# A decoder block's first conditioning columns loaded 256 wide, and its last addition and norm ordered by token tile

## The chip, the cores and the metric

The kernel runs on one core of a Trainium2 chip. The core has five engines that run side by side, each through its own instructions in order: TensorE (PE: products of matrices, into PSUM), VectorE (DVE), ScalarE (ACT), GpSimd (POOL) and SyncE (SP), which here issues most transfers. Sixteen DMA engines carry the transfers. The metric is the time of one execution on the device in microseconds (us), lower is better.

## The reference

The function is one block of a decoder on 512 tokens of 1024 channels, in float32, with a conditioning vector `c`:

```
mod = silu(c) @ w_ada + b_ada                      # 6 rows of 1024: sh1, sc1, g1, sh2, sc2, g2
h   = layer_norm(x) * (1 + sc1) + sh1
mix = hybrid_mixer(h, w_in, ...)                   # h @ w_in, state-space scan, short convolution, gates, w_o
x   = layer_norm(ALPHA * x + g1 * mix) * ln1_g + ln1_b
h   = layer_norm(x) * (1 + sc2) + sh2
ffn = moe_ffn(h, ...)                              # 64 experts, 8 per token, and one shared expert
x   = layer_norm(ALPHA * x + g2 * ffn) * ln2_g + ln2_b
```

The change touches the first two lines, as far as `sh1` and `sc1` go, and the last one.

## The kernel before

**Start.** The tokens are four tiles of 128 (`xt`), the channels eight chunks of 128. `x` is normed by token tile (`ln_stats`, L189 to L195, L258), and transposed by chunk. Before a chunk k can be scaled and shifted, its 128 columns of `sh1` and `sc1` must be known. `ada_cols(k)` loads these columns of `w_ada`, two tiles of 1024 x 128 (SP, L183, 512 KB each). `ada_mm(k)` multiplies them (L286): `csz` holds silu(c) in column 0 of 32, and the eight row blocks go to four groups of 32 columns of the array, each into its own 32 partitions of PSUM, so four products run side by side. ScalarE copies the result (L289). `h_chunk(k)` adds up the partitions with a product by ones (L294), adds the bias (L295), transposes the four token tiles (L150), scales and shifts (L300, into `hr`), splits `hr` into a rounded part and the rest (L158, L160), and multiplies it by the narrow columns for dt (L306, for two chunks at a time). The split parts feed `matmul3`, three products (L153 to L155) of a chunk of h with a chunk of four tiles of `w_in` (`first`), which are loaded and split beforehand. The loop runs over the eight chunks and keeps ada_mm and h_chunk one chunk ahead of the products.

Tiles of 1024 numbers per partition ("pages") come from 14 slots; a load waits until a slot is free. `am2` is one PSUM bank whose halves serve chunks in turn.

**Order.** A planner sets the order of the instructions on each engine from the program's order, its own costs and the times at which it expects operands; each engine then runs through its list in order. Only for TensorE in the expert stage the order is that of the program (`manual_schedule`).

**End.** The experts follow the mixer in units. The products of a unit's last block are added to the result `ra` by `csteps`, for the four token tiles in two halves of 512 columns (L1188 and L1189 into PSUM, L1194 adds; the last time L1191, which also gives the row sums). Before the change `combine(True)` runs all eight additions, and `finish` then norms: for each token tile a square with its sum (`square`: L1483 on VectorE, L1484 on ScalarE), the root (`root`: L1488, L1489) and the scaling and the store (`scale`: L1497 and L1498 on VectorE; for tile 0 L1492 on ScalarE and L1501, L1502 on GpSimd; the store at L1503). `FORD` is their order in the program. After that a loop for overflowing experts (L1510) follows, which makes no pass here; it holds a second call of both.

Of the kernel before, what the change touches and what calls it, by code (L numbers as in the profile page):

```python
# [8 lines left out]
F32 = mybir.dt.float32  # L9
# [4 lines left out]
OP = mybir.AluOpType  # L14
# [28 lines left out]
NDEF = 2  # L43
FORD = "q0 r0 s0 q1 r1 s1 q2 r2 s2 q3 r3 s3"
NADA = 3
# [18 lines left out]
def block_kernel(ctx: ExitStack, tc: tile.TileContext, a, out, dbg=None):  # L64
# [164 lines left out]

    def ada_cols(k):  # L230
        ws = []
        for i in range(2):
            ws.append(load_cols(a["w_ada"][0], i * D + k * P))
        return ws

    first = [C_X, C_X + P, C_B, C_C]
    awt = {0: ada_cols(0), 1: ada_cols(1)}
    wdt = work.tile([P, KD, NH], F32, name="wdt")
# [30 lines left out]
    dtp = bank("y", 2)  # L269
    am2 = bank("y", 2)  # L270
    fw, hrs = {}, {}
    ams = {}

    def ada_mm(k):
        if k + 2 < KD:
            awt[k + 2] = ada_cols(k + 2)
        if k == 0:
            win_load(first[2])
            win_load(first[3])
        am = am2[:, k % 2 * 256:k % 2 * 256 + 256]  # L280
        ws = awt.pop(k)
        for i in range(2):
            for half in range(2):
                for j in range(4):
                    kk = half * 4 + j
                    PE.matmul(am[32 * j:32 * j + 32, i * P:(i + 1) * P], csz[:, kk, :], ws[i][:, kk, :],  # L286
                              start=(half == 0), stop=(half == 1), tile_position=(0, 32 * j))
        ams[k] = wk()
        S.activation(ams[k][:, :256], am, AF.Copy)  # L289

    def h_chunk(k):
        am = am2[:, k % 2 * 256:k % 2 * 256 + 256]
        for i in range(2):
            PE.matmul(am[:, i:i + 1], ams[k][:, i * P:(i + 1) * P], ones[:, 0:1], start=True, stop=True)  # L294
        V.tensor_tensor(m1[:, k, :], am[:, :2], bcol[:, :, k], op=OP.add)  # L295
        tp = bank("tr", 2)
        for t in range(NT):
            transpose(tp[:, t * P:(t + 1) * P], xt[t][:, k * P:(k + 1) * P])
        hr = wk()
        V.tensor_scalar(hr, tp, m1[:, k, 1:2], m1[:, k, 0:1], op0=OP.mult, op1=OP.add)  # L300
        split_to(hh(k), hl(k), hr)
        hrs[k] = hr
        if k % DTG == DTG - 1:
            for q in range(k - DTG + 1, k + 1):
                j = q % 4
                PE.matmul(dtp[32 * j:32 * j + 32, :], wdt[:, q, :], hrs.pop(q), start=(q < 4), stop=(q >= 4),  # L306
                          tile_position=(0, 32 * j))
# [3 lines left out]
    for k in range(KD):  # L311
        if k + 1 < KD:
            ada_mm(k + 1)
        for i, c0 in enumerate(first):
# [881 lines left out]

    def combine(last=False):
        for _ in csteps(last):
            pass


# [208 lines left out]
    def unit(n):  # L1410
# [17 lines left out]
        drain(run)  # L1428

    over_ = iter(())  # L1430
    need_x(1)
# [4 lines left out]
    with tc.manual_schedule(engines={mybir.EngineType.PE}):  # L1436
        for n in range(MAN, len(units)):
            unit(n)
        combine(True)
    ostart, oend, obase, nov = far  # L1440
# [30 lines left out]

    ln2g, ln2b = page([D]), page([D])
    SY.dma_start(ln2g, bc_rows(a["ln2_g"], D))
    SY.dma_start(ln2b, bc_rows(a["ln2_b"], D))

    def finish():

        os_, st = {}, {}

        def square(t):  # L1480
            os_[t] = page([D])
            st[t] = const.tile([P, 4], F32, name="fst", bufs=4)
            V.tensor_scalar(st[t][:, 0:1], rsum[:, t, 0:1], rsum[:, t, 1:2], -1.0 / D, op0=OP.add, op1=OP.mult)  # L1483
            S.activation(os_[t], ra[t], AF.Square, bias=st[t][:, 0:1], scale=1.0, accum_out=st[t][:, 1:2])  # L1484

        def root(t):
            nmu, ss, rs, nb = (st[t][:, i:i + 1] for i in range(4))
            S.activation(rs, ss, AF.Sqrt, bias=epsc, scale=1.0 / D)  # L1488
            V.reciprocal(rs, rs)  # L1489
            if ENG3[t] != "VV":  # L1490
                V.tensor_tensor(nb, nmu, rs, op=OP.mult)
                S.activation(os_[t], ra[t], AF.Identity, bias=nb, scale=rs)  # L1492

        def scale(t):
            o, nmu, rs = os_[t], st[t][:, 0:1], st[t][:, 2:3]
            if ENG3[t] == "VV":
                V.scalar_tensor_tensor(o, ra[t], nmu, ln2g, op0=OP.add, op1=OP.mult)  # L1497
                V.scalar_tensor_tensor(o, o, rs, ln2b, op0=OP.mult, op1=OP.add)  # L1498
            else:
                e1, e2 = ({"V": V, "P": GP}[e] for e in ENG3[t])  # L1500
                e1.tensor_tensor(o, o, ln2g, op=OP.mult)  # L1501
                e2.tensor_tensor(o, o, ln2b, op=OP.add)  # L1502
            SY.dma_start(out[0, t * P:(t + 1) * P, :], o)  # L1503

        for c in FORD.split():
            {"q": square, "r": root, "s": scale}[c[0]](int(c[1]))

    finish()
    nv = nc.values_load(nov[0:1, 0:1], min_val=0, max_val=E + 32)
    with tc.For_i(0, nv, 1):  # L1510
# [3 lines left out]
        drain(expert([[0]], [[0]], [blk], [xsplit(blk[0])], lambda e, q: expert_piece(bass.ds(er, 1), q)))  # L1514
        combine(True)
        finish()
# [25 lines left out]
```

## Time and profile before

| | |
|---|---|
| time, three runs | median 1582.76 us (1582.29 to 1587.55) |
| profiled execution | 1580.36 us, span 1578.6 us |
| TensorE busy | 1486.1 us, 94% |
| VectorE busy | 975.3 us, 62% |
| ScalarE busy | 644.8 us, 41% |
| GpSimd busy | 227.3 us, 14% |
| moved by DMA | 335.67 MB, mean 213 GB/s |

The profiled execution is a run of its own; the span is the part of it between the first and the last instruction. Busy times are the sums of the instructions' spans on each engine. PE is the engine's products, PEld its loading of weights, which goes on beside the products.

### The profile page before, as it was taken

How to read it: one execution, taken by the hardware profiler on the slowest of the kernel's cores; microseconds unless marked ns; L12 is line 12 of the kernel's file. 1: busy time of each engine (PE TensorE's matmuls, PEld its weight loads, DVE VectorE, ACT ScalarE, POOL GpSimd, SP SyncE). 2: the span in 40 equal slices, each digit the busy share in tenths (PEclk: the TensorE clock that was granted, in tenths of full speed). 3: DMA queues.
4: the chain of work that ended last, by engine and by line, in shares of the span. 5: the costliest groups of instructions: out<-in, count | busy, mean ns of one | idle time of the engine just before them, and what ended most of it. 6: DMA issues, size and time to landing. Idle time of an engine off the chain costs nothing.

```text
span 1578.6 us, 22869 instructions
## 1 busy us (share of the span) xinstructions
PE 1486.1 (94%) x8253; PEld 1010.2 (64%) x8253; DVE 975.3 (62%) x1810; ACT 644.8 (41%) x925; POOL 227.3 (14%) x232
## 2 busy tenths in 40 slices
PE   6999989999999999999988999999988999999994
PEld 3688777787787886788766455555555554454552
DVE  4457786678767666635696666454566544563456
ACT  3456665575643445523353333232343322231222
POOL 0011110111010445700023300000000000000001
PEclk9999999999999999999999999999999999999997
DMA  9763423632531557634622967998989788997871
GB/s 278 183 158 91 104 67 84 151 77 80 151 88 37 170 178 231 202 101 148 228 84 92 370 224 260 375 383 296 345 299 349 293 332 336 353 365 282 319 286 55
DMA packets 194504, 335.67 MB, mean 213 GB/s; under 512 B 13428, under 2 KB 136660, under 8 KB 186196
## 3 DMA queue, kind: packets, MB, share of 16 engines
q1 hardware_dynamic: 183300, 303.73, 55.6%
q0 software_dynamic: 11088, 30.45, 7.4%
q8 instruction: 66, 1.08, 0.3%
q14 instruction: 50, 0.41, 0.1%
HBM read 334.58 MB, written 4.28 MB: 215 GB/s over the span
## 4 chain that ended last, share of the span: by engine, by line
PE 73%; DMA 11%; DVE 8%; ACT 3%; issue 2%; POOL 1%; SPq 1%; DVEq 0%; ACTq 0%; POOLq 0%
PE ps_pj L153 12%; PE ps_pj L154 12%; PE ps_pj L155 12%; PE ps_pj L950 8%; DMA pr<-in_w_up_dram 8%; PE ps_y L950 5%; PE ps_y L1188 5%; PE ps_y L1189 5%; PE ps_tr L150 4%; DMA pg<-in_w_ada_dram 2%; DVE wl L160 2%; PE ps_y L153 1%; PE ps_y L155 1%; PE ps_y L154 1%; PE ps_y L483 1%
## 5 line engine op out<-in xcount | busy, mean ns | idle before, releaser
L153 PE MATMUL ps_pj<-hm,wh 128*128 128x512 f32 x680 | 276.5, 408 | 1.0 <-ACT wh L158 0.9
L155 PE MATMUL ps_pj<-hm,wl 128*128 128x512 f32 x680 | 267.7, 394 | 6.3 <-DVE wl L160 6.3
L154 PE MATMUL ps_pj<-hm,wh 128*128 128x512 f32 x680 | 267.7, 394 | 0.0
L160 DVE TENSOR_TENSOR wl<-pg,wh 128x1024 fp32r<-128x1024 f32 (+1 forms) x129 | 159.6, 1244 | 114.0 <-ACT wh L158 113.9
L950 PE MATMUL ps_pj<-pr,xt 128*32 128x512 f32 (+1 forms) x1472 | 214.2, 604 | 11.9 <-DMA pr<-in_w_up_dram 11.7
L158 ACT ACTIVATE wh<-pg 128x1024 fp32r<-128x1024 f32 (+1 forms) x135 | 127.5, 953 | 137.3 <-PE ps_pj L154 101.6
L950 PEld LDWEIGHTS ps_pj<-pr,xt 128*32 128x32 f32 (+1 forms) x1472 | 62.0, 117 | 153.2 <-issue 149.6
L153 PEld LDWEIGHTS ps_pj<-hm,wh 128*128 128x128 f32 x680 | 129.1, 190 | 36.3 <-issue 6.9
L155 PEld LDWEIGHTS ps_pj<-hm,wl 128*128 128x128 f32 x680 | 128.6, 189 | 35.9 <-DVE wl L160 8.1
L154 PEld LDWEIGHTS ps_pj<-hm,wh 128*128 128x128 f32 x680 | 128.8, 189 | 29.1 <-issue 3.4
L160 DVE TENSOR_TENSOR wl<-pr,wh 128x1024 fp32r<-128x1024 f32 x72 | 86.8, 1222 | 85.9 <-ACT wh L158 85.4
L1194 DVE TENSOR_TENSOR res<-res,ps_y 128x512 f32<-128x512 f32 x120 | 82.4, 687 | 76.0 <-PE ps_y L1189 74.4
L1132 POOL DMA_INDIRECT pg<-h_d,idx x41 | 45.4, 1107 | 559.6 <-DVE oht L1161 174.3
L158 ACT ACTIVATE wh<-pr 128x1024 fp32r<-128x1024 f32 x72 | 74.3, 1054 | 91.2 <-DMA pr<-in_w_up_dram 54.5
L950 PE MATMUL ps_y<-pr,wkr 128*32 128x512 f32 (+1 forms) x736 | 102.7, 596 | 1.3 <-DVE wk L1165 1.3
L927 ACT ACTIVATE sg<-ps_pj 128x256 f32<-128x256 f32 x44 | 16.8, 383 | 173.7 <-PE ps_pj L950 116.4
L928 DVE TENSOR_TENSOR sg<-sg,ps_pj 128x256 f32<-128x256 f32 x44 | 18.3, 420 | 111.8 <-ACT sg L927 111.8
L366 POOL TENSOR_TENSOR pg<-pg 128x1024 f32<-128x1024 f32 x28 | 73.8, 2650 | 56.9 <-ACT pg L364 56.8
L153 PE MATMUL ps_pj<-pg,wh 128*128 128x512 f32 x192 | 75.9, 395 | 1.1 <-ACT zs L431 1.1
L155 PE MATMUL ps_pj<-pg,wl 128*128 128x512 f32 x192 | 76.2, 397 | 0.0
L154 PE MATMUL ps_pj<-pg,wh 128*128 128x512 f32 x192 | 75.8, 395 | 0.0
L416 DVE SCALAR_TENSOR_TENSOR wk<-ps_pj,cw,wk 128x511 f32<-128x511 f32 (+2 forms) x93 | 68.3, 742 | 7.4 <-ACT wk L414 7.0
(394 smaller groups left out, 2658.5 us busy)
## 6 DMA issues: line engine op xcount, KB each, us to landing
pr<-in_w_gate_dram SPq DMA_DIRECT2D x128, 512.0 KB, 10.1
pr<-in_w_up_dram SPq DMA_DIRECT2D x128, 512.0 KB, 10.6
pr<-in_w_down_dram SPq DMA_DIRECT2D x64, 1024.0 KB, 9.6
pg<-in_w_in_dram SPq DMA_DIRECT2D x88, 512.0 KB, 6.4
pg<-in_w_ada_dram SPq DMA_DIRECT2D x48, 512.0 KB, 3.5
bc<-acs_d POOLq DMA_DIRECT2D x32, 256.0 KB, 4.1
pg<-in_w_ssd_out_dram SPq DMA_DIRECT2D x16, 512.0 KB, 4.4
pg<-in_w_sc_out_dram SPq DMA_DIRECT2D x8, 512.0 KB, 4.0
```

What stands on the lines that cost most here:

```text
L150: return PE.transpose(o, i, ident[:n, :n])
L153: PE.matmul(o, lh, rh, start=start, stop=False)
L154: PE.matmul(o, lh, rl, start=False, stop=False)
L155: PE.matmul(o, ll, rh, start=False, stop=stop)
L158: S.activation(hi, src, AF.Copy)
L160: V.tensor_tensor(lo, src, rw(hi), op=OP.subtract)
L366: GP.tensor_tensor(part[i], part[i], w, op=OP.add)
L416: V.scalar_tensor_tensor(acc[:, s:], o[:, :T - s], cw[:, 3 - s, tl:tl + 1], acc[:, s:], op0=OP.mult, op1=OP.add)
L950: PE.matmul(o[w * i:w * i + w, :], x[:, w * i:w * i + w], m, start=start, stop=stop, tile_position=(0, w * i))
L1188: PE.matmul(o, oh_, yh[:, ns_], start=(i == 0), stop=False)
L1189: PE.matmul(o, oh_, yl[:, ns_], start=False, stop=(i == len(ps_) - 1))
L1194: V.tensor_tensor(ra[t][:, ns_], ra[t][:, ns_], o, op=OP.add)
```

## The change

The columns of `w_ada` for `sh1` and `sc1` are loaded for two chunks at once: for each of the two parts and each half of the rows one tile of 512 x 256, so that one piece in memory is 1 KB instead of 512 B. `ada_mm` runs for pairs of chunks, with 256 columns in one product, into one whole PSUM bank. The loads of the third and fourth tile of `w_in` are issued ahead of those of the next pair. At the end, `finish` stands inside the stretch with TensorE's manual order and takes the additions as steps of its own (c0 to c3, two halves each); FORD puts the squares, roots and scalings of the token tiles between them. The loads of `ln2_g` and `ln2_b` are in `finish`, at its first call.

```diff
-FORD = "q0 r0 s0 q1 r1 s1 q2 r2 s2 q3 r3 s3"
+FORD = "c0 q0 r0 s0 c1 q1 r1 c2 q2 r2 s1 c3 q3 r3 s2 s3"
...
-    def ada_cols(k):
-        ws = []
+    def ada_cols(kp):
+
+        ws = {}
         for i in range(2):
-            ws.append(load_cols(a["w_ada"][0], i * D + k * P))
+            for half in range(2):
+                v = ws[i, half] = page([4, 256])
+                SY.dma_start(v, a["w_ada"][0, half * 512:half * 512 + 512, i * D + kp * 256:i * D + kp * 256 + 256]
+                             .rearrange("(k p) n -> p k n", p=P))
         return ws
...
-    awt = {0: ada_cols(0), 1: ada_cols(1)}
+    awt = {0: ada_cols(0)}
...
-    def ada_mm(k):
-        if k + 2 < KD:
-            awt[k + 2] = ada_cols(k + 2)
-        if k == 0:
+    def ada_mm(kp):
+        if kp == 0:
             win_load(first[2])
             win_load(first[3])
-        am = am2[:, k % 2 * 256:k % 2 * 256 + 256]
-        ws = awt.pop(k)
+        if 2 * kp + 2 < KD:
+            awt[kp + 1] = ada_cols(kp + 1)
+        ws = awt.pop(kp)
         for i in range(2):
             for half in range(2):
                 for j in range(4):
-                    kk = half * 4 + j
-                    PE.matmul(am[32 * j:32 * j + 32, i * P:(i + 1) * P], csz[:, kk, :], ws[i][:, kk, :],
+                    PE.matmul(am[32 * j:32 * j + 32, i * 256:(i + 1) * 256], csz[:, half * 4 + j, :], ws[i, half][:, j, :],
                               start=(half == 0), stop=(half == 1), tile_position=(0, 32 * j))
-        ams[k] = wk()
-        S.activation(ams[k][:, :256], am, AF.Copy)
+        ams[kp] = wk()
+        S.activation(ams[kp], am, AF.Copy)

     def h_chunk(k):
-        am = am2[:, k % 2 * 256:k % 2 * 256 + 256]
+        kp, c = k // 2, k % 2
+        sums = am[:, 2 * c:2 * c + 2]
         for i in range(2):
-            PE.matmul(am[:, i:i + 1], ams[k][:, i * P:(i + 1) * P], ones[:, 0:1], start=True, stop=True)
-        V.tensor_tensor(m1[:, k, :], am[:, :2], bcol[:, :, k], op=OP.add)
+            PE.matmul(sums[:, i:i + 1], ams[kp][:, i * 256 + c * P:i * 256 + c * P + P], ones[:, 0:1], start=True, stop=True)
+        V.tensor_tensor(m1[:, k, :], sums, bcol[:, :, k], op=OP.add)
...
-        if k + 1 < KD:
-            ada_mm(k + 1)
+        if k % 2 and k + 1 < KD:
+            ada_mm(k // 2 + 1)
...
+    def finish():
+
+        if not ln2:
+            for nm in ("ln2_g", "ln2_b"):
+                ln2.append(page([D]))
+                SY.dma_start(ln2[-1], bc_rows(a[nm], D))
+        ln2g, ln2b = ln2
+        com = csteps(True)
+        os_, st = {}, {}
+
+        def add(t):
+            next(com)
+            next(com)
...
+            {"c": add, "q": square, "r": root, "s": scale}[c[0]](int(c[1]))
...
     with tc.manual_schedule(engines={mybir.EngineType.PE}):
         for n in range(MAN, len(units)):
             unit(n)
-        combine(True)
+        finish()
...
-    finish()
     nv = nc.values_load(nov[0:1, 0:1], min_val=0, max_val=E + 32)
     with tc.For_i(0, nv, 1):
...
-        combine(True)
         finish()
```

`square`, `root` and `scale` are the same in both.

## Rows read from the trace of the kernel before

**Rows 1.** Page, part 1: busy us, share of the span, instructions.

```profile
PE 1486.1 (94%) x8253; PEld 1010.2 (64%) x8253; DVE 975.3 (62%) x1810; ACT 644.8 (41%) x925; POOL 227.3 (14%) x232
```

**Rows 2.** Chain of waits, 0 to 80 us: start, us, what.

```profile
...
4.06 9.53 DMA pg<-in_w_ada_dram
...
```

**Rows 3.** Busy us of each engine by stretch, 12 to 75.6 us.

```profile
12.00:24.00 12.00, 10.46 (x85) 5.47 (x85) 5.67 (x13) 4.06 (x8) 0.00 (x0) 1.00 1.20 279
24.00:33.50 9.50, 8.26 (x57) 3.98 (x56) 5.53 (x8) 4.35 (x6) 0.00 (x0) 0.91 1.19 290
33.50:75.60 42.10, 42.10 (x319) 29.74 (x319) 17.32 (x31) 14.93 (x23) 0.00 (x0) 0.98 0.87 213
```

**Rows 4.** The same view, the end.

```profile
1557.30:1571.60 14.30, 0.00 (x0) 0.00 (x0) 12.18 (x15) 6.51 (x13) 5.55 (x2) 0.63 0.20 79
1571.60:1578.60 7.00, 0.00 (x0) 0.00 (x0) 0.00 (x0) 0.00 (x0) 0.00 (x0) 0.50 0.37 146
```

**Rows 5.** DMA view, 25 to 40 us.

```profile
DMA packets 8645, 4.36 MB, mean 290 GB/s; under 512 B 136, under 2 KB 8645, under 8 KB 8645
```

**Rows 6.** SyncE in order of time: start, us of all, what, how many.

```profile
13.41 3.41 SPq L183 DMA_DIRECT2D pg<-in_w_in_dram  x2
...
23.41 18.59 SPq L183 DMA_DIRECT2D pg<-in_w_ada_dram  x10
```

**Rows 7.** DMA view, 247 to 249 us, in 40 slices.

```profile
GB/s 205 307 348 369 348 389 348 348 430 328 348 410 389 430 369 348 369 389 389 410 369 369 369 389 287 103 62 61 41 0 0 0 0 0 0 0 0 0 0 0
DMA packets 471, 0.47 MB, mean 233 GB/s; under 512 B 16, under 2 KB 471, under 8 KB 471
```

**Rows 8.** TensorE in order of time: start, us, what, [idle before].

```profile
12.01 1.08 PE L286 MATMUL ps_y<-pg,csz 128*32 128x128 f32 x16
...
13.64 1.08 PE L286 MATMUL ps_y<-pg,csz 128*32 128x128 f32 x16
...
19.08 1.08 PE L286 MATMUL ps_y<-pg,csz 128*32 128x128 f32 x16
...
25.27 0.48 PE L153 MATMUL ps_pj<-hm,wh 128*128 128x512 f32 x1
...
29.35 0.50 PE L155 MATMUL ps_pj<-hm,wl 128*128 128x512 f32 x1
```

**Rows 9.** Groups of instructions, 0 to 80 us: count, busy us, mean ns, idle before.

```profile
L300 DVE TENSOR_SCALAR wk<-ps_tr,m 128x512 f32<-128x512 f32 x8 | 6.5, 810 | 1.7 <-PE ps_tr L150 1.5
...
L158 ACT ACTIVATE hm<-wk 128x512 fp32r<-128x512 f32 x8 | 5.1, 632 | 20.2 <-DVE wk L300 20.2
```

**Rows 10.** Chain of waits around chunk 7's columns.

```profile
59.91 1.01 PE ps_y L286 x32
60.92 0.43 PE ps_pj L153
61.36 0.24 PE ps_pj L154
...
63.36 0.98 PE ps_y L306 x2
```

**Rows 11.** TensorE in order of time, expert stage.

```profile
1484.60 11.36 PE L950 MATMUL ps_pj<-pr,xt 128*32 128x512 f32 x102
```

**Rows 12.** Single lines: count, min/median/max ns, first and last start.

```profile
L1191 DVE SCALAR_TENSOR_TENSOR res<-res,ps_y x8: 689/689/689, 1549.1 to 1556.6; 128x512 f32<-128x512 f32 x8
L1497 DVE SCALAR_TENSOR_TENSOR pr<-res,fst,pr x3: 1280/1285/3364, 1559.8 to 1563.7; 128x1024 f32<-128x1024 f32 x3
L1498 DVE SCALAR_TENSOR_TENSOR pr<-pr,fst x3: 1273/1285/3170, 1561.3 to 1570.3; 128x1024 f32<-128x1024 f32 x3
```

**Rows 13.** Groups of instructions of ScalarE, 1557 to 1579 us.

```profile
L1484 ACT ACTIVATE pr<-res,fst 128x1024 f32<-128x1024 f32 x4 | 4.5, 1138 | 7.5 <-DVE fst L1483 7.5
```

**Rows 14.** GpSimd in order of time, the end.

```profile
1563.65 2.35 POOL L1501 TENSOR_TENSOR pr<-pr 128x1024 f32<-128x1024 f32 x1 [91.36 <-ACT pr L1492]
1566.08 3.20 POOL L1502 TENSOR_TENSOR pr<-pr 128x1024 f32<-128x1024 f32 x1
```

More of the change, by code (lines that the diff above doesn't have):

```diff
@@ L269, in block_kernel @@
     dtp = bank("y", 2)
-    am2 = bank("y", 2)
+    am = bank("y", 2)
     fw, hrs = {}, {}
     ams = {}
-    def ada_mm(k):
-        if k + 2 < KD:
-            awt[k + 2] = ada_cols(k + 2)
-        if k == 0:
+    def ada_mm(kp):
+        if kp == 0:
             win_load(first[2])
             win_load(first[3])
-        am = am2[:, k % 2 * 256:k % 2 * 256 + 256]
-        ws = awt.pop(k)
+        if 2 * kp + 2 < KD:
+            awt[kp + 1] = ada_cols(kp + 1)
+        ws = awt.pop(kp)
         for i in range(2):
@@ L1195, in csteps @@
                 yield
-    def combine(last=False):
-        for _ in csteps(last):
-            pass
     out_proj(0)
@@ L1428, in unit, with square, root, scale @@
         drain(run)
+    ln2 = []
+    def finish():
[9 more added lines that the diff above has]
+            next(com)
+        def square(t):
+            os_[t] = page([D])
+            st[t] = const.tile([P, 4], F32, name="fst", bufs=4)
+            V.tensor_scalar(st[t][:, 0:1], rsum[:, t, 0:1], rsum[:, t, 1:2], -1.0 / D, op0=OP.add, op1=OP.mult)
+            S.activation(os_[t], ra[t], AF.Square, bias=st[t][:, 0:1], scale=1.0, accum_out=st[t][:, 1:2])
+        def root(t):
+            nmu, ss, rs, nb = (st[t][:, i:i + 1] for i in range(4))
+            S.activation(rs, ss, AF.Sqrt, bias=epsc, scale=1.0 / D)
+            V.reciprocal(rs, rs)
+            if ENG3[t] != "VV":
+                V.tensor_tensor(nb, nmu, rs, op=OP.mult)
+                S.activation(os_[t], ra[t], AF.Identity, bias=nb, scale=rs)
+        def scale(t):
+            o, nmu, rs = os_[t], st[t][:, 0:1], st[t][:, 2:3]
+            if ENG3[t] == "VV":
+                V.scalar_tensor_tensor(o, ra[t], nmu, ln2g, op0=OP.add, op1=OP.mult)
+                V.scalar_tensor_tensor(o, o, rs, ln2b, op0=OP.mult, op1=OP.add)
+            else:
+                e1, e2 = ({"V": V, "P": GP}[e] for e in ENG3[t])
+                e1.tensor_tensor(o, o, ln2g, op=OP.mult)
+                e2.tensor_tensor(o, o, ln2b, op=OP.add)
+            SY.dma_start(out[0, t * P:(t + 1) * P, :], o)
+        for c in FORD.split():
+            {"c": add, "q": square, "r": root, "s": scale}[c[0]](int(c[1]))
     over_ = iter(())
@@ L1470, in overflow @@
         return po, pv, ei
[L1472 to L1506, printed above, removed]
-    finish()
     nv = nc.values_load(nov[0:1, 0:1], min_val=0, max_val=E + 32)
```

## Prediction

> **What bounds the kernel now.** I read the page first, then the busy times by stretch, then the chain of waits, then single lines. TensorE is busy for 94% of the span [rows 1], so time is lost only where it waits or where it has nothing left to do. The change touches the two such places, at the start and at the end. (1) At the start the chain runs through a transfer of w_ada for 9.53 us, until 13.6 us [rows 2]. From 12 to 33.5 us TensorE is busy for 10.46 + 8.26 of 21.5 us and the DMA share stays at its ceiling (1.19 to 1.20). From 33.5 to 75.6 us it is busy for 42.10 of 42.10 us [rows 3]. So behind 33.5 us the start is bound by TensorE's own work, and an earlier arrival is worth exactly the work that TensorE has done more by then, plus what the rest becomes shorter. (2) At the end TensorE has nothing to do from 1557.3 us on. VectorE is busy for 12.18 of the next 14.30 us, and in the last 7.00 us no engine is busy: the last store and the close [rows 4], which nothing here changes.
>
> The profiled execution took 1580.36 us, 1.76 us more than its span; the runs have a median of 1582.76 us, 2.4 us above it. I work out a difference and subtract it from both.
>
> **Transfers of the start.** Each of the 16 loads is 512 KB before and after; the pieces grow from 512 B to 1 KB. With 512 B pieces, 8645 packets bring 4.36 MB in 15 us, 290 GB/s [rows 5], so 512 KB take 1.81 us, and SyncE's ten issues in 18.59 us (1.86 each) are paced by that [rows 6]. The trace has a stretch of 1 KB pieces (471 packets, 0.47 MB): 348 to 430 GB/s once it runs, about 365 [rows 7], so 1.44 us for 512 KB, 0.37 us less. Bounds for one load: 1.22 us (430) to 1.81 us (no gain). I take 1.44 because that row is of the very piece size.
>
> A page of the Trainium skill speaks against this: "DMA: Bandwidth & Descriptors", Specifications, gives 512 B as the least transfer for line rate. By it 512 B pieces already run at full rate and the loads would take 1.81 us as before. The rows differ (290 against about 365 GB/s), and I go by the rows; what it would make of the time is rival A.
>
> Arrival, in issue order. Before, the first two w_ada loads released TensorE at 12.01 and 13.64 us [rows 8]. After, four loads are needed before the first pair of chunks is complete: 11.6 + 3 x 1.44 = 16.0 us, 2.4 us later than 13.64. The first two w_in loads follow at about 18 and 20 us (before, 13.41 us [rows 6] plus about 6.4 us to landing is 19.8), and now w_in three and four come next, at about 21.7 and 23.5, ahead of the next four w_ada loads, which end at 23.5 + 4 x 1.44 = 29.3 us. Two of these four need pages (14 in all: 4 x, 4 w_ada, 4 w_in, so 2 left), which the first ada_mm frees at about 17 us; SyncE stands at them with only later loads behind, and the transfers queued ahead last until 23.5, so that wait costs nothing.
>
> **TensorE's work by then.** First chunk, after: four loads at 16.0, last products 0.9, copy about 0.6, sums 1.0 and 0.16, then L300 at about 19 to 20 us. The second chunk now needs no load and no copy of its own and follows at once. With L300 0.81 and the copy 0.63 behind it [rows 9], the first products of matmul3 (three to a call) start at about 22 us, against 25.27 us before [rows 8]. All four w_in tiles are there by 23.5, so chunks 0 and 1 (24 products of 0.23 us, and four of L306 at 0.49 [rows 10]) fill 22 to 29.5 us. Then ada_mm(1) ends at about 30, and L300 of chunks 2 and 3 runs at 31.6 to 33.2. TensorE idles about 1.5 us there; before, it idled 1.24 us between 24 and 33.5 [rows 3].
>
> At 33.5 us TensorE had before done 12 such products, the first at 25.27 and the last at 29.35 us [rows 8]. After, it has done 24: 12 x 0.23 = 2.8 us ahead; and chunk 3's share of ada_mm: 1.0 us [rows 10]. Against that stands one chunk of L306 not yet done: 0.98. Net -2.8 us.
>
> The rest gets shorter too. A chunk's ada_mm is 32 records in 1.01 us, and the product behind it takes 0.43 instead of 0.24 us [rows 10]. After, two chunks are 32 records of 256 columns. From below, if a record's price didn't depend on its columns, 1.01 us for two chunks; from above 2.02. The nearest row with four column groups side by side has 102 records of 512 columns in 11.36 us, 0.111 each [rows 11], so 0.056 for 256 columns and 1.78 us for 32. I take that: 0.24 us less per pair, and one 0.2 us switch less. Of four pairs, two and a half lie behind 33.5 us: -1.2 us (bounds 0 and -3). The single bank `am` makes ada_mm(kp+1) wait for the addition of the second chunk's sums; in program order six products and that chunk's transposes and L306 stand between, so it is over by then, and I cost it at nothing. Uncovered it would be the addition and its wait, under 0.3 us each time.
>
> Front: -2.8 - 1.2 = -4.0 us (bounds +1 to -6). All that follows moves with it, since the start ends in a stretch where TensorE never waits [rows 3].
>
> **The end.** Before: eight additions of 0.69 us [rows 12], the last ending at 1557.3; then squares on ScalarE (1.14 us each [rows 13]), with VectorE waiting 2.1 us for them; then L1497 and L1498 for three tiles, 1.28 us each undisturbed, 7.7 us. One L1497 took 3.36 and one L1498 3.17 us [rows 12]: they start inside GpSimd's L1501 and L1502 [rows 14]; the first, begun at 1563.7, ends one microsecond after L1501. Over 1.28 each, 4.0 us are waiting. The additions read PSUM; all eight took 0.69.
>
> After: statistics and squares of tiles 0 to 2 run between the additions, so the 2.1 us go. FORD puts s1 (2 x 1.28) ahead of c3, so the last addition ends about 2.6 us later, and another 1.0 us for the small instructions moved ahead of it. Behind it stand 0.2 for q3, s2 (2.6 us, which covers the square of tile 3), and s3 (2.6): 5.4 us. Without collisions: 1557.3 + 3.6 + 5.4 = 1566.3 instead of 1571.6, -5.3. GpSimd's 2 x 2.35 us for tile 0 now fall at about 1556.5 to 1562, onto s1, and stop it for 2 to 4 us, as they stop tiles 2 and 3 now. Part of them falls on the PSUM additions, which they don't stop. That gives -1.3 to -3.3; I take -2.5. If VectorE kept strictly to FORD, each r would hold the next additions for the square's 1.14 us and the small steps behind it, which I estimate at 0.6, so 1.75 us, three times: 1557.3 + 5.2 + 2.6 + 1.75 + 5.1 = 1572.0, +0.5 to +1. The planner didn't keep to it before (all four q stood first), so I take that as the upper end. ln2's loads and the four stores keep their queue and their order; the last store still follows the last L1498.
>
> **Sum:** -4.0 - 2.5 = -6.5 us: 1573.9 for a profiled execution, 1576.3 for the median, 0.41% less.
>
> **Rivals.**
> A. 1 KB pieces bring no rate. For: rows 7 show one load by itself, and no row shows 1 KB pieces in a long queue. Against: its rate holds over most of that load. Then the second w_ada group ends at 29.3 + 8 x 0.37 = 32.3 us, 3 us later, and eats the 2.8: front -1.2, total -3.7, 1579.1. Chance 0.12.
> B. The end stays as long: VectorE waits for each tile's root, +0.5 to +1, with the front as forecast: total -3, 1579.8. Chance 0.15.
> C. The other side: the planner sets ada_mm(1) ahead of the products of chunks 0 and 1, as it set chunk 1's (the last at 19.08) ahead of chunk 0's products before [rows 8], and TensorE, in order, stands from about 22 until 29.3 us. The 24 products and four of L306 (7.5 us) come after it: front +3.5, and with the end -2.5 total +1, 1583.8; with B as well +4. It decides if the planner takes the transfers for more than 4 us earlier than they are. For: those loads now stand behind 2 MB of w_in. Against: before, only the first two loads were waited for. Chance 0.10.
> D. More: ada_mm's records cost nearly the same at 256 columns, or GpSimd falls wholly onto additions: -10 to -12, about 1571.5. Chance 0.13.
> Forecast: 0.50, between 1572 and 1580.
>
> Below 0.5% (7.9 us) a change of this kernel can't be told from none: runs of before differ by 5 us. Faster by more than that: D and the lower part of the forecast, 0.35. Slower by more: the tail of C, or orders planned anew in the stages between, 0.08. Range 1570 to 1586, from D's end to beyond C.
>
> **What would show it.** 1 KB packets at 350 GB/s or more up to 30 us; TensorE's first product of matmul3 at about 22 us instead of 25.27; 24 of them by 33.5; L286 at about 1.8 us per 32 records; the start's dense stretch ending about 4 us earlier; the last L1498 about 9 us after the last addition of tile 2. Wrong: w_ada landing later than 30 us with TensorE idle, or VectorE idle between the last additions.

## The result, and the profile after

The changed kernel takes 1577.5 us, median of 11 runs (1568.71 to 1583.3); the kernel before takes 1583.2 us in 11 runs (1576.31 to 1590.42). The ratio is 0.9942 with a 95% interval of 0.992 to 0.9963: about 9 us less by the ratio (the medians are 5.7 us apart), against a forecast of 6.5. A second measurement of the same kernel gave 0.9939 (0.9914 to 0.9964).

The profiled execution of the changed kernel is its slowest run: 1583.3 us, span 1581.5 us, 2.9 us more span than the profiled one of before: the mean granted clock of that run is 0.978 (before: 0.983), and the expert stage alone, which the change does not touch, took 717.7 us in it instead of 706.4, with the same 4264 TensorE records. So the two spans cannot be subtracted; I compare stage by stage.

Busy times by stretch, before and then after (length; busy us and count of PE, PEld, DVE, ACT, POOL; granted clock, DMA share, GB/s):

```profile
842.70:1549.10 706.40, 670.39 (x4264) 371.45 (x4262) 388.29 (x730) 207.08 (x329) 62.10 (x53) 0.99 0.82 310
```

```profile
838.00:1555.70 717.70, 676.25 (x4264) 376.46 (x4262) 388.47 (x731) 207.03 (x330) 62.11 (x53) 0.98 0.81 305
```

TensorE has 8125 records after, 128 fewer than in [rows 1]: half of the 256 of ada_mm.

**The start, after.** The same three stretches as in [rows 3]:

```profile
12.00:24.00 12.00, 10.71 (x52) 3.31 (x52) 7.60 (x16) 6.49 (x9) 0.00 (x0) 0.90 1.18 298
24.00:33.50 9.50, 9.50 (x63) 5.94 (x62) 3.26 (x3) 1.14 (x2) 0.00 (x0) 0.94 1.09 348
33.50:75.60 42.10, 40.82 (x236) 26.97 (x229) 19.75 (x37) 17.34 (x25) 0.00 (x0) 1.00 0.72 193
```

From 24 to 33.5 us TensorE is busy throughout (before: 8.26 of 9.50), with a granted clock of 0.94. The stretch behind it, full before, now has 1.28 us of idle time. TensorE in order of time shows where (start, us, what, [idle before]):

```profile
20.66 1.05 PE L309 MATMUL ps_y<-wk,wdt 128*32 128x512 f32 x2 [0.24 <-DVE wk L303]
...
22.24 1.92 PE L309 MATMUL ps_y<-wk,wdt 128*32 128x512 f32 x2
...
24.86 0.59 PE L153 MATMUL ps_pj<-hm,wh 128*128 128x512 f32 x1
...
32.84 0.40 PE L155 MATMUL ps_st<-hm,pg 128*128 128x512 f32 x1
33.17 0.64 PE L288 MATMUL ps_y<-pg,csz 128*32 128x256 f32 x8
34.53 0.61 PE L297 MATMUL ps_y<-ones,wk 128*128 128x1 f32 x4 [0.72 <-ACT wk L291]
35.46 0.61 PE L297 MATMUL ps_y<-ones,wk 128*128 128x1 f32 x4 [0.32 <-DVE m L298]
36.30 1.04 PE L309 MATMUL ps_y<-wk,wdt 128*32 128x512 f32 x2 [0.24 <-DVE wk L303]
```

The first product of matmul3 starts at 24.86 us, hardly before the 25.27 of [rows 8] and not at 22; but 24 of them are through by 33.24 us, as forecast, where before had 12. ada_mm(1)'s four groups stand among these products (the last at 33.17), so TensorE did not stand in front of them.

SyncE in order of time and the DMA view from 25 to 36 us, after:

```profile
10.49 8.25 SPq L183 DMA_DIRECT2D pg<-in_w_in_dram  x4
18.79 17.08 SPq L236 DMA_DIRECT2D pg<-in_w_ada_dram  x12
```

```profile
DMA packets 3838, 3.83 MB, mean 348 GB/s; under 512 B 114, under 2 KB 3837, under 8 KB 3837
```

Twelve loads of 512 KB take 17.08 us, 1.42 us each (forecast 1.44; 1.86 in [rows 6]), at 348 GB/s instead of the 290 of [rows 5].

**A fair mark for the start.** The forecast's mark, the end of the start's dense work, I read first at the last dt product: 66.1 us before, 62.3 after, 3.8 earlier. That mark is uneven: before, 83 products of matmul3 stand ahead of it, after only 76; seven at 0.23 us are 1.6 us. So I count products (the records of L153, L154 and L155 in order of their starts): at the 100th, every product of ada_mm, of the sums and of dt is done in every trace.

| trace | start of the kernel | last dt product (products ahead) | 100th product | 200th product | from the first of the last eight additions to the span's end |
|---|---|---|---|---|---|
| before | before | 66.1 (83) | 70.6 | 98.4 | 29.5 |
| e2_tail_only | before | 67.0 (83) | 71.6 | 99.3 | 25.1 |
| after | changed | 62.3 (76) | 68.2 | 92.1 | 25.8 |
| e11_changed_again | changed | 62.5 (76) | 68.4 | 92.2 | 25.8 |
| e1_front_only | changed | 64.0 (76) | 69.9 | 93.7 | 29.3 |
| e5_no_gpsimd | changed | 62.2 (76) | 68.2 | 92.0 | 24.9 |
| e6_s1_last | changed | 61.3 (76) | 67.2 | 91.0 | 26.4 |
| e9_best | changed | 63.3 (76) | 69.2 | 93.1 | 24.1 |
| e3_pieces_512, e3_again | 512 B pieces | 63.1, 64.6 (76) | 69.0, 70.5 | 92.8, 94.3 | - |
| e4_columns_128 | 128 columns | 63.6 (79) | 69.1 | 93.2 | 26.0 |
| e7_columns_first | old load order | 67.2 (79) | 72.6 | 96.7 | 25.8 |
| e8_win_first | before, new load order | 61.9 (83) | 66.4 | 90.2 | 29.4 |
| e10_swap_and_end | before, new load order | 64.9 (83) | 69.4 | 93.2 | 24.2 |

By the 100th product the six traces of the changed start are 2.6 us ahead of the two of before (68.5 against 71.1, means; the six spread over 2.7 us). By the 200th they are 6.5 us ahead (92.3 against 98.8). Between these two counts lies a wait of before that the forecast never looked at. Busy times there, before and after:

```profile
75.60:80.00 4.40, 2.65 (x12) 1.58 (x11) 3.96 (x8) 4.23 (x8) 0.00 (x0) 0.96 0.01 2
80.00:90.00 10.00, 10.00 (x41) 8.04 (x40) 6.36 (x13) 7.29 (x8) 0.00 (x0) 0.85 0.00 0
```

```profile
75.60:80.00 4.40, 4.40 (x21) 3.65 (x20) 4.37 (x8) 4.32 (x7) 0.00 (x0) 1.00 0.01 2
80.00:90.00 10.00, 10.00 (x48) 8.29 (x47) 5.33 (x11) 7.59 (x10) 0.77 (x1) 1.00 0.12 28
```

Before, TensorE idles 1.75 us directly behind the stretch where [rows 3] ended, and then has a granted clock of 0.85: part of the next ten microseconds is run at 1.2 GHz after that idling, which costs as much again. In 14.4 us it does 53 records instead of 69. TensorE in order of time, before:

```profile
77.76 0.40 PE L154 MATMUL ps_pj<-hm,wh 128*128 128x512 f32 x1
79.44 0.66 PE L155 MATMUL ps_y<-hm,wl 128*128 128x512 f32 x1 [1.29 <-DVE wl L160]
79.90 0.63 PE L153 MATMUL ps_y<-hm,wh 128*128 128x512 f32 x1
```

It waits 1.29 us for VectorE's first subtraction of a split (wl, L160), after 0.47 us for ScalarE's rounded part of another (wh, L158). VectorE in order of time, then ScalarE, before:

```profile
69.60 4.70 DVE L416 SCALAR_TENSOR_TENSOR wk<-ps_pj,cw,wk 128x511 f32<-128x511 f32 x7 [1.78 <-ACT wk L414]
...
78.17 1.21 DVE L160 TENSOR_TENSOR wl<-pg,wh 128x1024 fp32r<-128x1024 f32 x1
```

```profile
71.45 2.02 ACT L158 ACTIVATE wh<-pg 128x1024 fp32r<-128x1024 f32 x2
```

The same two after:

```profile
67.02 1.22 DVE L160 TENSOR_TENSOR wl<-pg,wh 128x1024 fp32r<-128x1024 f32 x1 [4.44 <-ACT wh L158]
68.17 4.68 DVE L419 SCALAR_TENSOR_TENSOR wk<-ps_pj,cw,wk 128x511 f32<-128x511 f32 x7
```

```profile
65.93 1.06 ACT L158 ACTIVATE wh<-pg 128x1024 fp32r<-128x1024 f32 x1 [2.31 <-PE ps_pj L154]
```

Not one line of that code differs, only the order on VectorE and ScalarE: before, the convolution's steps (on VectorE seven in the first row, more behind them; on ScalarE L414) stand ahead of the first split; after, the split stands ahead of them. Of all the traces only the two with the start of before have the old order here, so the planner set this part anew when the start ahead of it was another; why it did is not shown.

**The end, after.** The last additions, the two scaling lines (count, min/median/max ns, first and last start), GpSimd, and VectorE in order of time:

```profile
L1194 DVE SCALAR_TENSOR_TENSOR res<-res,ps_y x8: 668/688/691, 1555.7 to 1564.3; 128x512 f32<-128x512 f32 x8
```

```profile
L1462 DVE SCALAR_TENSOR_TENSOR pr<-res,fst,pr x3: 1265/1276/3184, 1563.0 to 1572.4; 128x1024 f32<-128x1024 f32 x3
```

```profile
L1463 DVE SCALAR_TENSOR_TENSOR pr<-pr,fst x3: 1285/1285/2891, 1564.9 to 1573.7; 128x1024 f32<-128x1024 f32 x3
```

```profile
1564.36 2.35 POOL L1466 TENSOR_TENSOR pr<-pr 128x1024 f32<-128x1024 f32 x1 [84.94 <-ACT pr L1457]
1566.79 3.21 POOL L1467 TENSOR_TENSOR pr<-pr 128x1024 f32<-128x1024 f32 x1
```

```profile
1564.31 0.67 DVE L1194 SCALAR_TENSOR_TENSOR res<-res,ps_y 128x512 f32<-128x512 f32 x1
...
1564.90 2.89 DVE L1463 SCALAR_TENSOR_TENSOR pr<-pr,fst 128x1024 f32<-128x1024 f32 x1
...
1567.90 3.18 DVE L1462 SCALAR_TENSOR_TENSOR pr<-res,fst,pr 128x1024 f32<-128x1024 f32 x1
1571.12 1.28 DVE L1463 SCALAR_TENSOR_TENSOR pr<-pr,fst 128x1024 f32<-128x1024 f32 x1
```

From the first of the last eight additions to the end of the span it takes 25.8 us instead of 29.5: 3.7 us less. The 2.1 us that VectorE waited for squares are gone; two scalings still run inside GpSimd's two instructions, 2.89 and 3.18 us instead of 1.28, together 3.5 us (4.0 in [rows 12]). The addition at 1564.31 ran inside L1466 as well and took its usual 0.67.

### The profile page after: what moved, and what is told of

Its sections match the earlier page's. It is cut to its first block, busy times and chain, and to the rows that moved or that the text cites. A ratio compares the mean times of both kernels' runs of the same rounds, so it can differ in the third digit from the quotient of the medians.

```text
span 1581.5 us, 22600 instructions
## 1 busy us (share of the span) xinstructions
PE 1488.8 (94%) x8125; PEld 1010.5 (64%) x8125; DVE 973.6 (62%) x1810; ACT 644.8 (41%) x921; POOL 227.4 (14%) x232
## 4 chain that ended last, share of the span: by engine, by line
PE 71%; DMA 13%; DVE 9%; ACT 3%; issue 2%; POOL 2%; SPq 1%; ACTq 0%; DVEq 0%; POOLq 0%
PE ps_pj L153 12%; PE ps_pj L154 12%; PE ps_pj L155 12%; DMA pr<-in_w_up_dram 8%; PE ps_pj L953 7%; PE ps_y L953 5%; PE ps_y L1191 5%; PE ps_y L1192 5%; PE ps_tr L150 4%; DVE wl L160 2%; DMA od<-acs_d 2%; PE ps_y L153 1%; DMA pg<-in_w_ada_dram 1%; PE ps_y L154 1%; POOL pg L369 1%
## 5 line engine op out<-in xcount | busy, mean ns | idle before, releaser
L153 PE MATMUL ps_pj<-hm,wh 128*128 128x512 f32 x680 | 276.2, 407 | 1.8 <-ACT wh L158 1.5
L155 PE MATMUL ps_pj<-hm,wl 128*128 128x512 f32 x680 | 268.2, 395 | 4.8 <-DVE wl L160 4.8
L154 PE MATMUL ps_pj<-hm,wh 128*128 128x512 f32 x680 | 267.8, 394 | 0.0
L160 DVE TENSOR_TENSOR wl<-pg,wh 128x1024 fp32r<-128x1024 f32 (+1 forms) x129 | 158.8, 1237 | 115.9 <-ACT wh L158 115.8
L158 ACT ACTIVATE wh<-pg 128x1024 fp32r<-128x1024 f32 (+1 forms) x135 | 127.3, 952 | 135.7 <-PE ps_pj L154 107.1
L153 PEld LDWEIGHTS ps_pj<-hm,wh 128*128 128x128 f32 x680 | 129.0, 190 | 37.9 <-issue 7.1
L155 PEld LDWEIGHTS ps_pj<-hm,wl 128*128 128x128 f32 x680 | 128.6, 189 | 35.2 <-DVE wl L160 7.1
L154 PEld LDWEIGHTS ps_pj<-hm,wh 128*128 128x128 f32 x680 | 129.0, 190 | 28.7 <-issue 2.6
L160 DVE TENSOR_TENSOR wl<-pr,wh 128x1024 fp32r<-128x1024 f32 x72 | 86.7, 1220 | 88.5 <-ACT wh L158 88.0
L158 ACT ACTIVATE wh<-pr 128x1024 fp32r<-128x1024 f32 x72 | 74.3, 1053 | 92.4 <-DMA pr<-in_w_up_dram 63.1
L153 PE MATMUL ps_pj<-pg,wh 128*128 128x512 f32 x192 | 75.9, 395 | 2.8 <-ACT zs L434 2.8
L155 PE MATMUL ps_pj<-pg,wl 128*128 128x512 f32 x192 | 76.2, 397 | 0.0
L154 PE MATMUL ps_pj<-pg,wh 128*128 128x512 f32 x192 | 75.8, 395 | 0.0
```

What stands on the lines that cost most here:

```text
L153: PE.matmul(o, lh, rh, start=start, stop=False)
L154: PE.matmul(o, lh, rl, start=False, stop=False)
L155: PE.matmul(o, ll, rh, start=False, stop=stop)
L158: S.activation(hi, src, AF.Copy)
L160: V.tensor_tensor(lo, src, rw(hi), op=OP.subtract)
```

## The experiments

**The two halves alone.**

```diff
# e1_front_only: the changed kernel, its end as before
-FORD = "c0 q0 r0 s0 c1 q1 r1 c2 q2 r2 s1 c3 q3 r3 s2 s3"
+FORD = "q0 r0 s0 q1 r1 s1 q2 r2 s2 q3 r3 s3"   # behind combine(True)
# e2_tail_only: the kernel before with the new FORD and finish()
```

> The start of the changed kernel (columns by pairs, 256 wide), the end of the kernel before. Theory (two separate gains that add up): the first instruction behind the last dt product, ScalarE's L668 of the kernel before, starts at 63.0 us as in the changed kernel (66.8 before); the expert stage starts 4 to 5 us earlier than before; the stretch from the first last-addition to the end of the span stays at 29.5 us; time 4 to 5 us less, ratio about 0.997. Rival (the expert stage is paced by its transfers and gives back what the start gains): same mark at 63.0, but the last additions start no earlier than before and the ratio is 1.000.

> The start of the kernel before, the end of the changed kernel. Theory: the mark behind the last dt product stays at 66.8 us; from the first last-addition to the end of the span 25.8 us instead of 29.5; time 3.6 us less, ratio about 0.998. Rival (the gain of the end hangs on what the start moved, such as when the ln2 rows land): 29 us or more, ratio 1.000.

Measured: the start alone 0.9982 (0.9951 to 1.0012), the end alone 0.9987 (0.9965 to 1.0009), each in 10 runs. Both intervals hold 1: neither half can be told from no change by its time, and by the point estimates they add to 5 us, not 9. The traces are sharper: the start alone has the 200th product 5.1 us before the mean of before's start (93.7 against 98.8), and its end is the old one (29.3 us); the end alone has the start of before (99.3) and an end of 25.1 us. So the two gains are there separately and do not need each other. That the times show less than the marks lies within their intervals.

**The size of the pieces.** The same loads in the same places of every queue, 128 columns by 1024 rows in 512 B pieces instead of 256 by 512 in 1 KB pieces.

```diff
# e3_pieces_512, run again as e3_again
-SY.dma_start(v, a["w_ada"][0, half * 512:half * 512 + 512, i * D + kp * 256:i * D + kp * 256 + 256]
-             .rearrange("(k p) n -> p k n", p=P))
+SY.dma_start(v.rearrange("p k (c n) -> p (k c) n", c=2), a["w_ada"][0, :, i * D + (2 * kp + half) * P:
+             i * D + (2 * kp + half) * P + P].rearrange("(k p) n -> p k n", p=P))
```

> The changed kernel, with each of the 16 loads of w_ada fetched as 1024 rows of 128 columns (512 B in one piece) instead of 512 rows of 256; every engine's instructions and their order are those of the changed kernel. The numbers land in another place, so the first scale and shift aren't the reference's. Theory (the rate of the pieces is worth something): the 12 later issues of SyncE take about 1.8 us each instead of 1.42, the second group lands about 3 us later, and the mark behind the last dt product, 63.0 us in the changed kernel, comes at 64.5 to 66. Rival (the order alone brought the gain of the start): the mark stays at 63.0 within 0.3, whatever the issues take.

> The 512 B kernel once more, since one trace has one sample of the clock in the first 62 us. The first time the mark came at 63.1, 0.8 later than in the changed kernel. If the rate counts for 1 to 2 us, the mark is again 0.8 to 2 us behind the mean of the changed start's samples; if it counts for nothing, it lies among them.

SyncE in order of time, and the busy times of the stretch, with 512 B pieces:

```profile
19.06 22.84 SPq L236 DMA_DIRECT2D pg<-in_w_ada_dram  x12
```

```profile
24.00:36.00 12.00, 11.17 (x68) 6.01 (x66) 3.88 (x5) 2.34 (x3) 0.00 (x0) 1.00 1.21 291
```

The rate goes back as it should: 1.90 us for a load instead of 1.42, 291 GB/s instead of 348. The time hardly follows: the last dt product is at 63.1 and 64.6 us, the 100th product at 69.0 and 70.5, mean 69.75, 1.2 us behind the changed start's 68.5 where I had given the rate the greater part of the front's 4.0. The two traces are 1.5 us apart and the changed start's six spread over 2.7, so even the 1.2 us is not clear of the scatter. Only the start is comparable here; the total (1801.25 us) is that of other tokens going to the experts.

**The width of the products.** Two groups of 128 columns in place of one of 256.

```diff
# e4_columns_128
-            for half in range(2):
-                for j in range(4):
-                    PE.matmul(am[32 * j:32 * j + 32, i * 256:(i + 1) * 256], csz[:, half * 4 + j, :], ws[i, half][:, j, :],
...
+            for c in range(2):
+                for half in range(2):
+                    for j in range(4):
+                        PE.matmul(am[32 * j:32 * j + 32, i * 256 + c * P:i * 256 + c * P + P], csz[:, half * 4 + j, :],
+                                  ws[i, half][:, j, c * P:c * P + P],
...
```

> The changed kernel, with each product of 256 columns of w_ada as two of 128; loads as in the changed kernel, order planned anew. Theory (columns set the price): a pair's products take 2.0 us instead of 1.86, and the mark behind the last dt product moves by 0.5 us or less, to 63.0 to 63.5. Rival (width saves TensorE 1.2 us or more, as the prediction's term had it): the mark comes at 64.2 or later.

One pair of chunks in the chain of waits, the changed kernel and then this one:

```profile
53.16 1.86 PE ps_y L288 x32
```

```profile
53.74 1.88 PE ps_y L289 x64
```

32 records of 256 columns cost what 64 of 128 do. The width buys 0.02 us a pair; against the 2 x 1.01 of [rows 10] a pair is 0.14 to 0.16 us shorter in either shape. The 100th product (69.1) is 0.5 us behind the mean of the changed start, within its spread.

**The order of the loads.** In ada_mm the change also moves the third and fourth w_in load ahead of the next columns. First the changed kernel without that, then the kernel before with nothing but that.

```diff
# e7_columns_first: the changed kernel
 def ada_mm(kp):
+    if 2 * kp + 2 < KD:
+        awt[kp + 1] = ada_cols(kp + 1)
     if kp == 0:
         win_load(first[2])
         win_load(first[3])
-    if 2 * kp + 2 < KD:
-        awt[kp + 1] = ada_cols(kp + 1)
# e8_win_first: the kernel before
 def ada_mm(k):
+    if k == 0:
+        win_load(first[2])
+        win_load(first[3])
     if k + 2 < KD:
         awt[k + 2] = ada_cols(k + 2)
-    if k == 0:
-        win_load(first[2])
-        win_load(first[3])
```

> The changed kernel with the second pair's columns issued ahead of the third and fourth w_in tile, the order of the kernel before. Theory (the gain of the start is that chunk 1 follows chunk 0 without a load and a copy of its own): those two w_in tiles land about 6 us later, the second pair 3.6 us earlier, and the mark behind the dt products stays within 62.0 to 64.0. Rival (the earlier w_in tiles feed TensorE while it waits for the second pair): TensorE idles 3 us or more between 24 and 36 us and the mark comes at 65 or later.

> The kernel before, with one edit: the third and fourth w_in tile are issued ahead of chunk 2's columns instead of behind them; columns by single chunks, 512 B pieces and 128 columns as before. Theory (what the start gains is mostly the place of these two loads): the mark behind the last dt product, 66.1 and 67.0 with the start of the kernel before and 61.3 to 64.0 with the changed one, comes at 63 to 64.5. Rival (the place counts only with columns by pairs, which free chunk 1 from a load of its own): 66 to 67.

With the old order the changed kernel has its 100th product at 72.6 us: 4.1 later than with the new one and 1.5 later than before's. SyncE in order of time and the busy times:

```profile
24.16 2.66 SPq L338 DMA_DIRECT2D vr<-in_ssd_conv_w_dram  x1
...
30.82 8.24 SPq L236 DMA_DIRECT2D pg<-in_w_ada_dram  x8
```

```profile
24.00:36.00 12.00, 10.72 (x68) 5.91 (x67) 4.88 (x8) 5.05 (x7) 0.00 (x0) 0.89 0.81 213
36.00:62.00 26.00, 24.71 (x144) 14.04 (x144) 5.94 (x14) 3.50 (x6) 0.00 (x0) 0.92 0.73 212
```

It is no long stop of TensorE, as I had thought it might be: 1.28 us idle in the first stretch and 1.29 in the second. Its last eight w_ada loads are issued only from 30.82 us, the DMA share falls to 0.81 in the stretch where the changed kernel has 1.09, and part of the records behind these waits runs at the lower clock (0.89 and 0.92 granted; the changed kernel has 0.95 and 1.00). So this one trace does not price the order of the two loads alone: the planner also set seven small loads (from L338 at 24.16 to L667 at 30.29 us) ahead of those eight, whereas in the kernel before and in the changed one they come behind all loads of w_ada, and the lower clock by itself is worth about 3 us here (an estimate from the granted clocks of the two traces, 12 to 62 us).

The kernel before with only the two loads moved has its 100th product at 66.4 us and its 200th at 90.2: the whole gain of the changed start and more, with 512 B pieces and 128 columns, and with the rest of SyncE's loads up to 45 us in before's order. It took 1571.24 us in one run, beside 1585.55 of before. Its VectorE, too, has the first wl (66.14 us) ahead of the convolution, so the planner's other order comes with every start that differs from before's:

```profile
66.14 1.22 DVE L160 TENSOR_TENSOR wl<-pg,wh 128x1024 fp32r<-128x1024 f32 x1 [1.85 <-ACT wh L158]
67.28 4.68 DVE L416 SCALAR_TENSOR_TENSOR wk<-ps_pj,cw,wk 128x511 f32<-128x511 f32 x7
```

**GpSimd at the end.** All tiles on VectorE; and s1 behind the last addition.

```diff
# e5_no_gpsimd (run again, timed, as e9_best)
-ENG3 = ("PP", "VV", "VV", "VV")
+ENG3 = ("VV", "VV", "VV", "VV")
# e6_s1_last
-FORD = "c0 q0 r0 s0 c1 q1 r1 c2 q2 r2 s1 c3 q3 r3 s2 s3"
+FORD = "c0 q0 r0 s0 c1 q1 r1 c2 q2 r2 c3 q3 r3 s1 s2 s3"
```

> The changed kernel with token tile 0 scaled on VectorE as the other three, GpSimd left out at the end; TensorE's order is the same, so the start is one more sample of the changed start (mark behind the dt products 62.3 there). Theory (VectorE's long scalings wait for GpSimd): all eight scalings take 1.26 to 1.30 us, none over 1.4; the end, from the first last-addition to the close of the span, changes by -3.5 (the waits of 1.6 and 1.9) + 2.6 (two more scalings), 25.8 to about 25. Rival (something else holds them, such as the stores or ScalarE): some still take about 3 us, and the end grows to 28.4.

> The changed kernel with s1 behind c3 in FORD: all eight additions ahead of all scalings on VectorE. Theory (what counts is on what GpSimd's two instructions fall): the last addition comes about 2 us earlier, but both GpSimd instructions now fall on scalings, which wait 3.5 to 4.5 us in all; end 25.5 to 27 us. Rival (s1 ahead of c3 holds up tile 3, which ends last): end 24.5 us or less.

> The changed kernel with token tile 0 scaled on VectorE, timed against the kernel before. If start (-4.1 us by the marks) and end (-4.6 by the traces) both reach the total, the ratio is 0.9945 (0.993 to 0.996). If the expert stage gives back the start's part, 0.997.

The scaling lines of the first, then of the second:

```profile
L1462 DVE SCALAR_TENSOR_TENSOR pr<-res,fst,pr x4: 1271/1276/1285, 1557.6 to 1567.2; 128x1024 f32<-128x1024 f32 x4
...
L1463 DVE SCALAR_TENSOR_TENSOR pr<-pr,fst x4: 1262/1276/1284, 1559.4 to 1568.6; 128x1024 f32<-128x1024 f32 x4
```

```profile
L1462 DVE SCALAR_TENSOR_TENSOR pr<-res,fst,pr x3: 1259/1268/3354, 1552.3 to 1560.2; 128x1024 f32<-128x1024 f32 x3
```

```profile
L1463 DVE SCALAR_TENSOR_TENSOR pr<-pr,fst x3: 1272/1273/3256, 1553.6 to 1562.6; 128x1024 f32<-128x1024 f32 x3
```

Without GpSimd no scaling is stretched (1.26 to 1.29 us), and the end takes 24.9 and 24.1 us although VectorE does 2.6 us more: the long ones were GpSimd's doing. With s1 last the two collisions cost 4.1 us (3.35 + 3.26 less 2 x 1.27) and the end 26.4 us. Timed, the changed kernel with all tiles on VectorE has 0.9932 (0.9904 to 0.996) in 7 runs: a gain over the changed kernel's 0.9942 and 0.9939 that these intervals can't show.

The Trainium skill ("SBUF — State Buffer", Who interferes with whom) says that a VectorE instruction with two SBUF inputs contends with a GpSimd instruction that reads SBUF, over a shared pair of ports that one of them locks. The traces agree: 2.89 to 3.36 us inside GpSimd's instructions and 1.27 outside. It goes both ways: in e6 GpSimd's L1466 begins at 1552.93 us, inside VectorE's scaling of 1552.29 to 1553.56, and takes 2.83 us; in the changed kernel no scaling runs at its start, and it takes 2.35. The addition, which reads PSUM, takes 0.67 inside them.

**The best parts together.** The kernel before with the two loads moved and the new end, all tiles on VectorE; neither pairs nor 1 KB pieces. Beside it the changed kernel again.

```diff
# e10_swap_and_end: e8's edit, FORD and finish() of the change, and
-ENG3 = ("PP", "VV", "VV", "VV")
+ENG3 = ("VV", "VV", "VV", "VV")
# e11_changed_again: the changed kernel, no edit
```

> The kernel before with two edits: the third and fourth w_in tile issued ahead of chunk 2's columns, and the changed end with token tile 0 on VectorE. No columns by pairs, no 1 KB pieces. Theory (the place of the two loads carries the gain of the start): the mark behind the last dt product at 61.5 to 63.5, the end 24 to 25 us, ratio to the kernel before 0.993 to 0.996, not slower than the changed kernel beside it. Rival (the 61.9 of the swap alone was a favourable clock, and pairs and pieces are worth 1 to 2 us): the mark at 64 or later, and a time above the changed kernel's.

> The changed kernel itself, beside the run above on one chip, as a second sample of its trace: mark behind the last dt product 62 to 63.5, end 25 to 26 us, ratio to the kernel before 0.994 to 0.996.

It takes 1571.56 us (7 runs; ratio 0.9908, 0.9875 to 0.9942) beside 1576.2 of the changed kernel (12 runs; 0.9939, 0.9914 to 0.9964) and 1584.2 of before. The means of the two, 1570.5 and 1575.6, differ by 5.1 us with a standard error of 1.8 (from the spreads of 3.7 and 4.3 us); part of this may be the granted clock of its runs, 0.985 in the mean against 0.982. That it beats the kernel before is shown; that it beats the changed kernel is likely.

Its start missed: the 100th product at 69.4 us with the very code that had 66.4 in e8. TensorE in order of time, e8 and then e10:

```profile
11.51 1.08 PE L286 MATMUL ps_y<-pg,csz 128*32 128x128 f32 x16
...
19.93 1.05 PE L306 MATMUL ps_y<-wk,wdt 128*32 128x512 f32 x2
...
22.69 1.04 PE L306 MATMUL ps_y<-wk,wdt 128*32 128x512 f32 x2 [0.89 <-DVE wk L300]
...
24.07 0.47 PE L153 MATMUL ps_pj<-hm,wh 128*128 128x512 f32 x1
```

```profile
12.38 1.08 PE L286 MATMUL ps_y<-pg,csz 128*32 128x128 f32 x16
...
21.10 1.92 PE L306 MATMUL ps_y<-wk,wdt 128*32 128x512 f32 x2
...
25.13 1.92 PE L306 MATMUL ps_y<-wk,wdt 128*32 128x512 f32 x2 [0.64 <-DVE wk L300]
...
27.74 0.69 PE L153 MATMUL ps_pj<-hm,wh 128*128 128x512 f32 x1
```

Two things of the single execution: the first product with the columns starts 0.87 us later, and the same pair of records takes 1.92 us instead of 1.05, twice, up to 27 us. The granted clock reads 1.00 from 12 to 28 us in both, so that column does not show it and its cause is open. These marks of one code lie 3 us apart, so a mark of the start from one trace is good to about 1.5 us either way.

## Why the prediction came out as it did

The total was close (1576.3 forecast, 1577.5 measured) and lies in the range; the gain, 0.58%, is a little beyond the 0.5% that I had called "no change" and thought likelier. But the sum is right in part by luck: terms were mis-sized and one failed, and the errors cancel.

- **"512 KB take 1.44 us": right.** 1.42 us. Rival A's premise, that 1 KB brings no rate, is wrong. The rule that the prediction set beside it (the Trainium skill, "DMA: Bandwidth & Descriptors", Specifications: 512 B is the least transfer for line rate) does not fit these runs: 290 and 291 GB/s at 512 B, 348 at 1 KB.
- **"24 products by 33.5 us": right; "net -2.8 us" at that point: mis-sized.** By [rows 8] and the rows after, 12 products (2.8 us) and one chunk's share of ada_mm (1.0) are done more. Not yet done is one chunk of dt (0.98), and also that chunk's sums (0.34), which I left out; the transposes of the first four chunks are through by 25.8 us in both. And the 1.5 us of idle time, which I had in front of 33.5 us, came behind it (1.28 us), because the first product started at 24.86 and not 22: chunk 1's dt products, at 1.92 us instead of 1.04, were set ahead of it. 2.8 + 1.0 - 0.98 - 0.34 - 1.28 leaves 1.2 us.
- **"The rest gets shorter, -1.2": mis-sized.** Two pairs ran behind 33.5 us, not two and a half (the chunk's share above is the other half), and a pair is 0.16 us shorter in the records (forecast 0.24), not by their width: 0.3 us. The 0.2 us switch is priced by no run. A further 0.8 us, which I had not thought of, is an estimate from the clock of the same stretch, 42.1 us at 1.00 instead of the 0.98 of [rows 3]. Together with the 1.2 that is 2.3 us; measured, the trace after is 2.4 us ahead of the trace before at the 100th product, against 4.0.
- **What brings it: the step gave the wrong cause.** The prediction derived the front from pairs and faster arrival; the new load order stands in its timeline without a price of its own. In e8 and e10 the order alone gives 3.1 us at the 100th product (mean of 66.4 and 69.4 against 71.1) and 7.1 at the 200th (91.7 against 98.8), as much as the whole changed start (2.6 and 6.5). At the 100th that is two traces 3 us apart; at the 200th it is clear of their scatter. In e7 pairs and 1 KB pieces with the old order gain nothing at the 100th (1.5 us behind before), but in one trace with a low clock and small loads moved, so what they are worth by themselves stays open. The rate is worth about 1.2 us within the changed kernel, not clear of the scatter, the width nothing that can be seen.
- **"All that follows moves with it, since the start ends in a stretch where TensorE never waits": failed, to the good side.** The window of [rows 3] ended at 75.6 us. At 75.6 begins before's next wait, 1.75 us of idling and a slower stretch behind it; from the 100th to the 140th product before needs 13.5 us in both of its traces, every other start 9.6. These 3.9 us are more than the dense start gave, and I had put "orders planned anew" only on the slower side. That the wait can go was to be read from the trace of before: VectorE's row at 78.17 stands behind the convolution's steps, for which the trace shows nobody waiting.
- **"Between the start and the end nothing changes": not settled.** The lead of the changed start is 6.5 us at the 200th product and 4.5 at the 2800th, shortly before the expert stage, where the six traces spread with a standard deviation of 2.4; in the expert stage single executions differ by up to 13 us (704.2 to 717.7). A small give-back there can neither be shown nor excluded. The lead of 4.5 to 6.5 and the end's 3.7 make 8 to 10 us, and the timed ratio is 9.2 us (5.9 to 12.7).
- **The end, "-2.5": right in kind, 1.2 us too little.** Measured 3.7 (means of 29.4 and 25.7). The squares' wait goes as described; the collisions cost 3.5 us, where I allowed 2 to 4 and took 2.8. From the first addition's start to the last one's end it takes 9.31 us instead of 8.15, 1.2 more where I set 3.6: the planner put only one of s1's two scalings (at 1563.0 us) ahead of the last addition, not both as in FORD, and VectorE idles 0.4 us less between the additions. Behind the last addition stand 6.5 us without the collisions, where I set 5.4. And from the last scaling to the end of the span, where I had nothing change, the traces with the new end and GpSimd take 6.5 to 6.7 us (the two with 512 B pieces apart, where other tokens go to the experts), those with the old end 7.0; the cause of that is open. Rival B (the roots hold VectorE) did not happen: up to the last addition VectorE's gaps, for TensorE or none, are 0.6 us at most.
- **Rival C** (the planner sets ada_mm(1) ahead of the products) did not happen: its groups start at 29.24, 30.23, 31.46 and 33.17 us, among them. **Rival D** had its size of total nearly (9 against 10 to 12) but by neither of its two reasons: records of 256 columns cost twice those of 128, and GpSimd did not fall onto the additions alone.

## What to carry to other kernels

Where loads share one queue in order and few buffers, ask first which load the dense work needs next; here their order alone moved the 100th product by about 3 us and the 200th by about 7, their rate the 100th by about 1.2, within the scatter. When work is moved under a planner, read the trace of the old kernel beyond the stretch that you change, up to the next wait: its order there is set anew as well, and what stands in that wait is a term of the sum with either sign. And measure a gain by a count of equal work (the 100th, the 200th product), not by the time of one instruction that may have changed places.

## What the runs showed of the hardware

- GpSimd's instruction stops a VectorE instruction of two SBUF operands to its end (2.89 to 3.36 us instead of 1.27) and is itself held by one that began earlier (2.83 us instead of 2.35 for the same line); one that reads PSUM is left alone (0.67).
- A wait of TensorE of 1.3 us was followed by records at the lower level: 0.63 us for a product that takes 0.39 to 0.40, until 83 us, with 0.85 granted from 80 to 90. The idle time (1.75 us with the 0.47 ahead of it) was a little under half of what that stretch cost (3.9 us).
- ada_mm's products, four column groups side by side, cost by their columns: 64 records of 128 columns 1.88 us, 32 of 256 columns 1.86.
- The same code in the same place had the pair of dt records at 1.05 us in one execution and 1.92 in another, with a granted clock of 1.00 from 12 to 28 us in both.
